# A low weight part formed by an accumulating DMA in every fourth half of a two-layer encoder's weight stream

## The chip, the cores and the metric

The kernel runs on one core of a Trainium2 chip. The metric is the device time of one execution in microseconds. The kernel before takes 2125.69 us (median of 3 runs, 2125.62 to 2129.74).

## What is computed

The reference is a two-layer encoder on one sequence of 256 tokens with 2048 features, in float32. Cut to what matters:

```python
for i in range(DEPTH):                      # DEPTH = 2
    h = rms_norm(x, attn_norm[i])
    if i % 2 == 0:                          # 8 heads on a 64-wide grid, 8 dilated heads
        x = x + even_mixer(h, even_w_in[j], even_rpb[j], even_w_out[j])
    else:                                   # 16 query heads, 4 key/value heads, window 128
        x = x + odd_mixer(h, odd_w_qkv[j], odd_sink[j], odd_w_out[j])
    x = x + sq_relu_mlp(rms_norm(x, mlp_norm[i]), w_mlp_in[i], w_mlp_out[i])
return rms_norm(x, final_norm)
```

All weights are used once. They make up most of the 382 MB that the kernel reads from HBM.

## The kernel before, in words

**Two exact parts.** Every float32 operand of a matmul is split in two: a high part that ScalarE (ACT) makes by copying to the type float32r, and a low part that VectorE (DVE) makes as the operand minus its high part (`split`, L80 to L82). A product is then three products: high by high, high by low, low by high. The activations keep their two parts side by side (`u`, `hid`, `o`, each with features on the partitions).

**The weight stream.** A unit is 16 tiles (k-tiles) of 128 x 128 weights, one output tile of 128 features. It comes in two halves of 8 k-tiles, 512 KB each. `need` puts the halves of all matrices on one list in the order of their use; `take_half` (L94 on) takes the next. It first fills a queue of loaded halves up to `AHEAD` + 1, and for each of these it issues the load on SP's queue (L98, tile `r`, 6 buffers), the copy `h<-r` on ACT (L81, 5 buffers) and the subtraction `l<-r,h` on DVE (L82, 5 buffers). `AHEAD` is 2. Of twelve units, the first ones after a phase in which activations become ready late, the second half has only 6 k-tiles in `h` and `l`; its last two go to tiles of their own.

**The products.** `k_range` (L134 on) issues two matmuls per k-tile on TensorE (PE): `h` against both activation parts at once (512 columns, L142) and `l` against the high part (256 columns, L144). `value_pair` (L253 on) uses the weights as the moving operand and works on two halves at a time (L264). `unit` takes a sum bank of three, `joined` empties it (ACT L171, DVE L173). Small work of attention and of the norms is put off by `later` and issued between k-tiles.

**Order.** The code's order is a priority: the framework plans times for all instructions when the program is built, and writes each engine's queue in the order of that plan. An instruction whose inputs are planned to be ready earlier can stand ahead of one that comes before it in the code (POOL issues `rev<-in_rpb`, L495, ahead of `sink_neg`, L448). On the chip each queue is then worked off strictly in its written order.

**The start.** Three units are loaded and multiplied in step with the activations (L440 to L465). GpSimd (POOL) loads small tables (L444 to L447). Before and between the first pairs of heads it makes the grid's bias for 8 heads, `make_grid_bias`: two loads `rev` on POOL's own DMA queue (L495, one buffer), then `rel<-rev,mask_a` (L497, four buffers), which waits for these. After the eighth `rel` POOL has no work. `norm_for_heads` makes the first norm: sums on PE (L202), the root on ACT (L205), a few small steps and a diagonal matrix on DVE (L213), then a product with it on PE (L217).

Of the kernel before, what the change touches and what calls it, by code (L numbers as in the profile page):

```python
# [7 lines left out]
F32 = mybir.dt.float32  # L8
F32R = mybir.dt.float32r
AF = mybir.ActivationFunctionType  # L10
ALU = mybir.AluOpType
# [15 lines left out]
HALF = KT // 2  # L27
RAW_BUFS = 6
PART_BUFS = 5
# steps between the stages of a head's attention  # L30
LAGS_0 = (5,4,3)
LAGS_1 = (4,5,3)
LAGS_END = (3,3,2)
# [7 lines left out]
def encoder(ctx: ExitStack, tc: tile.TileContext, a: dict, outT: bass.AP):  # L41
    nc = tc.nc
# [6 lines left out]
    work = ctx.enter_context(tc.tile_pool(name="work", bufs=3))  # L49
    acc_ps = ctx.enter_context(tc.tile_pool(name="acc_ps", bufs=3, space=PSUM))  # L50
    aux_ps = ctx.enter_context(tc.tile_pool(name="aux_ps", bufs=1, space=PSUM))

# [1 line left out]
    xs = const.tile([P, KT, T], F32, name="xs")  # L54
    u = const.tile([P, KT, 2, T], F32R, name="u")
    g = const.tile([P, 5, KT], F32, name="g")
# [15 lines left out]
    nc.vector.memset(eps, EPS)  # L72

    def warm(func, after):
        # has the function's table loaded ahead of its use
        nc.scalar.activation(warmed, after, func)

    warm(AF.Sqrt, eps)
# [1 line left out]
    def split(hi, lo, src):  # L80
        nc.scalar.activation(hi, src, AF.Copy)  # L81
        nc.vector.tensor_sub(lo, src, hi.bitcast(F32))  # L82

# [1 line left out]
    AHEAD = 2  # L85
    pending = []
    loaded = []

    def need(units, held=0):
        # of the first `held` units the last two k-tiles get tiles of their own  # L90
        for i, src in enumerate(units):
            pending.extend([(src[:, :HALF, :], HALF), (src[:, HALF:, :], HALF - 2 if i < held else HALF)])

    def take_half():  # L94
        while pending and len(loaded) <= AHEAD:
            src, n = pending.pop(0)
            r = raw.tile([P, HALF, P], F32, name="r")
            nc.sync.dma_start(r, src)  # L98
            h = whi.tile([P, HALF, P], F32R, name="h")
            l = wlo.tile([P, HALF, P], F32R, name="l")  # L100
            split(h[:, :n, :], l[:, :n, :], r[:, :n, :])
            tiles = [(h[:, k, :], l[:, k, :]) for k in range(n)]
            if n < HALF:
                h, l = (held_w.tile([P, 2, P], F32R, name=name) for name in ("hh", "hl"))
                split(h, l, r[:, n:, :])
                tiles += [(h[:, k, :], l[:, k, :]) for k in range(2)]
            loaded.append((h, l, tiles))
        return loaded.pop(0)

    def take_unit():  # L110
        return take_half()[2] + take_half()[2]

# [1 line left out]
    now = [0]  # L114
    tasks = []

# [8 lines left out]
    def tick():  # L125
        now[0] += 1
        run_due()

    def finish_tasks():
        while tasks:  # L130
            now[0] = max(now[0], tasks[0][0])
            run_due()
# [19 lines left out]
        done(ps)  # L152

    def some_units(done, act):
        # the last k-tiles of the activations become ready late: leave them for the end
        ps = [acc_ps.tile([P, 2 * T], F32, name="acc") for _ in done]
        parts = []
        for i in range(len(done)):
            parts.append(take_unit())
            if act is not u:  # L160
                assert heads_done >= set(range(KT - 2))
            k_range(ps[i], parts[i], act, range(KT - 2))
        if act is not u:
            finish_tasks()
        for i in range(len(done)):
            k_range(ps[i], parts[i], act, range(KT - 2, KT))
            done[i](ps[i])
# [5 lines left out]
        nc.vector.tensor_add(z, ps[:, :T], t)  # L173
        return z

# [1 line left out]
    def gained(k, which):  # L177
        x, gk = xs[:, k, :], g[:, which, k:k + 1]
        if which == 4:
# [14 lines left out]
    norm = {"ready": False, "waiting": []}  # L194

    def finish_norm(last=None, to=None):
        # mean square with tokens on partitions, 1/rms there, and the same along every partition
        ps = aux_ps.tile([P, 512], F32, name="m_ps", bufs=2)
        parts = [ssq] if last is None else [ssq, last]
        for j in range(2):  # L200
            for n, part in enumerate(parts):
                nc.tensor.matmul(ps[:, j:j + 1], part[:, j * P:(j + 1) * P], ones[:, 0:1],  # L202
                                 start=n == 0, stop=n == len(parts) - 1)
        r0, v, e = (work.tile([P, 2], F32, name=n, bufs=1) for n in ("r0", "v", "e"))
        nc.scalar.activation(r0, ps[:, :2], AF.Sqrt, bias=eps, scale=1.0 / D)  # L205
        nc.vector.tensor_scalar(v, ps[:, :2], 1.0 / D, EPS, op0=ALU.mult, op1=ALU.add)
        nc.vector.reciprocal(r0, r0)
        nc.vector.scalar_tensor_tensor(e, r0, -0.5, r0, op0=ALU.mult, op1=ALU.mult)
        nc.vector.tensor_mul(e, e, v)
        nc.vector.scalar_tensor_tensor(rcol, e, 1.5, r0, op0=ALU.add, op1=ALU.mult)  # L210
        diag = work.tile([P, 2, P], F32, name="diag", bufs=1)
        for j in range(2):
            nc.vector.tensor_scalar(diag[:, j, :], ident, rcol[:, j:j + 1], None, op0=ALU.mult)  # L213

        def along():
            out = aux_ps.tile([P, 512], F32, name="m_ps", bufs=2)
            nc.tensor.matmul(out[:, :T], ones, diag.rearrange("p j t -> p (j t)"), start=True, stop=True)  # L217
            to(out[:, :T])
        return along
# [13 lines left out]
        later(2, finish_norm(to=to))  # L233
        norm["ready"] = False

# [1 line left out]
    def head_parts(pool, name, bufs, scale, keep):  # L237
        def done(ps):
            z = joined(ps)
# [11 lines left out]
        return done  # L251

    def value_pair(pool, keep):  # L253
        # tokens on partitions, two heads at a time
        ps = acc_ps.tile([P, 2, T], F32, name="acc")
        for half in range(2):
            parts = [take_half()[:2] for _ in range(2)]
            for kk in range(HALF):
                k = half * HALF + kk
                h, l = (w.rearrange("p k c -> p (k c)")[:, (kk % 4) * T:(kk % 4 + 1) * T] for w in parts[kk // 4])  # L260
                for j in range(2):
                    js = slice(j * P, (j + 1) * P)
                    for n, (x, y) in enumerate(((0, h), (0, l), (1, h))):
                        nc.tensor.matmul(ps[:, j, :], u[:, k, x, js], y,  # L264
                                         start=k == 0 and j == 0 and n == 0,
                                         stop=k == KT - 1 and n == 2, skip_group_check=True)
                if kk % 2 == 1:
                    tick()
        assert norm["ready"]
        w = pool.tile([P, 2, 2, T], F32R, name="v", bufs=1)  # L270
        for j in range(2):
            nc.scalar.activation(w[:, 0, j, :], ps[:, j, :], AF.Copy, scale=rcol[:, j:j + 1])
            nc.vector.scalar_tensor_tensor(w[:, 1, j, :], ps[:, j, :], rcol[:, j:j + 1],
                                           w[:, 0, j, :].bitcast(F32), op0=ALU.mult, op1=ALU.subtract)
        keep.append(w)

    def attend(pool, o, head, q, k, v, side, biases, lags, sunk=False):
        """q, k, v: lists that hold the operands once their units are done."""
        def scores():
            if not q or not k:  # L280
                later(1, scores)
# [120 lines left out]
                    final = which_next == 4 and b == 1 and c == KT - 1  # L402
                    unit(added(c, final), hid, srcs=2, summed=final)

# [1 line left out]
    w0, w1 = a["even_w_in"], a["odd_w_qkv"]  # L406
    for p in range(8):
        base = 2 * p if p < 4 else 24 + 2 * (p - 4)
# [16 lines left out]
    need([a["odd_w_out"][c] for c in range(KT)], 3)  # L425
    mlp_units(1)

# [1 line left out]
    wps = aux_ps.tile([P, 512], F32, name="m_ps", bufs=2)  # L429
    for _ in range(10):  # L430
        nc.tensor.matmul(wps[:, :P], ones, ones, start=True, stop=True)

# [1 line left out]
    STARTERS = 3  # L434
    GROUPS = ((0, 2), (2, 4), (4, 8), (8, 12), (12, 16))
    starters = [[pending.pop(0)[0] for _ in range(2)] for _ in range(STARTERS)]
# [13 lines left out]
    for k0, k1 in GROUPS:  # L450
# [9 lines left out]
        for i in range(STARTERS):  # L460
            h, l = hl[i]
            for k in range(k0, k1):
                nc.tensor.matmul(sps[i], h[:, k % HALF, :], u[:, k].rearrange("p a t -> p (a t)"),
                                 start=k == 0, stop=False)
# [9 lines left out]
        later(1 + gi, some_squares(gi))  # L474
    later(8, norm_for_heads)

# [1 line left out]
    with tc.tile_pool(name="attn0", bufs=1) as pool:  # L478
        o = pool.tile([P, NH, 2, T], F32R, name="o")
        sl = slopes(8)  # L480
# [22 lines left out]
        for p in range(8):  # L503
            q, k, v = [[], []], [[], []], []
            for i in range(2):
                for j, (dst, name, sc) in enumerate(((q, "q", SCALE), (k, "k", 1.0))):
                    done = head_parts(pool, name, 2, sc, dst[i])
# [4 lines left out]
                h = 2 * p + i  # L512
# [7 lines left out]
        finish_tasks()  # L520
    mlp(0, 2)

# [1 line left out]
    with tc.tile_pool(name="attn1", bufs=1) as pool:  # L524
        o = pool.tile([P, NH, 2, T], F32R, name="o")
        sl = slopes(16)
        for p in range(2):
            k, v = [[], []], []
            done = [head_parts(pool, "k", 2, 1.0, k[i]) for i in range(2)]
# [7 lines left out]
            for i in range(8):  # L537
                h = 8 * p + i
                q = []
# [15 lines left out]

    mlp(1, 4)

# [1 line left out]
    def to(r):  # L559
        for k0, k1 in ((0, 1), (1, 2)) + tuple((k, k + 2) for k in range(2, KT, 2)):  # L560
            ks = slice(k0, k1)
            nc.vector.tensor_mul(xs[:, ks, :], xs[:, ks, :], r[:, None, :].to_broadcast([P, k1 - k0, T]))  # L562
            nc.sync.dma_start(outT[:, ks, :], xs[:, ks, :])
# [68 lines left out]
```

## Time and profile before

| | |
|---|---|
| median of 3 runs | 2125.69 us |
| the profiled execution | span 2127.8 us from first to last instruction (it has no other time of its own) |
| PE / PEld busy | 2104.8 us (99%) / 1852.0 us (87%) |
| DVE busy | 1340.4 us (63%) |
| ACT busy | 1035.6 us (49%) |
| POOL busy | 23.2 us (1%) |
| share of 16 DMA engines, loads on SP's queue | 53.2% |
| chain that ended last | PE 96%, DMA 2%, DVE 1% |

PE is TensorE's matmuls and PEld its weight loads, which overlap them. The chain is followed back from the last instruction to what released each step; its shares tell which engine the end depends on.

### The profile page before, as it was taken

The page shows a single profiled execution, that of the slowest core. Times are in us where ns is not written, and L with a number is a line of the kernel's source. Part 1 is how long each engine was busy: PE and PEld are TensorE (multiplying, and loading weights), DVE is VectorE, ACT ScalarE, POOL GpSimd, SP SyncE. Part 2 cuts the span into 40 slices and gives each one's busy share as a digit, 9 for nine tenths or more (in the row PEclk, how much of TensorE's full clock was granted, in tenths as well). Part 3 has the DMA queues.
Part 4 walks back from the last instruction along what each step waited for, and adds up shares of the span by engine and source line. Part 5 has one row for each costly group of instructions (what it writes and reads, how often), then busy time and mean ns, then how long its engine had stood idle before and what let it go on. Part 6 is the DMA issues. An engine that isn't in the chain of part 4 may idle for free.

```text
span 2127.8 us, 31825 instructions
## 1 busy us (share of the span) xinstructions
PE 2104.8 (99%) x12438; PEld 1852.0 (87%) x12438; DVE 1340.4 (63%) x2088; ACT 1035.6 (49%) x1602; POOL 23.2 (1%) x33
## 2 busy tenths in 40 slices
PE   8999999999999999999999999999999999999997
PEld 6999998888888888888888998888888888888887
DVE  6766676766655556665656877766655556665554
ACT  6555555544444444444445656544444444444442
POOL 2100000000000000000000000000000000000000
PEclk9999999999999999999999999999999999999998
DMA  9754455555555555555555444555555555555552
GB/s 258 180 171 168 168 170 176 190 180 188 187 187 188 188 186 185 187 187 189 188 188 187 148 162 143 188 185 188 185 187 187 188 188 186 187 188 188 188 188 90
DMA packets 108294, 386.06 MB, mean 181 GB/s; under 512 B 12352, under 2 KB 13392, under 8 KB 108144
## 3 DMA queue, kind: packets, MB, share of 16 engines
q1 hardware_dynamic: 106992, 381.73, 53.2%
q0 software_dynamic: 1008, 2.27, 1.5%
q8 instruction: 97, 1.59, 0.3%
q14 instruction: 53, 0.43, 0.1%
q10 hardware_dynamic: 144, 0.04, 0.0%
HBM read 381.89 MB, written 2.10 MB: 180 GB/s over the span
## 4 chain that ended last, share of the span: by engine, by line
PE 96%; DMA 2%; DVE 1%; SPq 0%; ACT 0%; issue 0%; DVEq 0%; ACTq 0%
PE acc L142 58%; PE acc L144 30%; PE acc L264 5%; PE s_ps L288 1%; PE m_ps L332 1%; DMA r<-in_even_w_in 1%; PE p_ps L313 1%; DMA r<-in_even_w_v 1%; DMA xs<-in_xT 0%; ACT h L81 0%; DVE l L82 0%; DVE xs L562 0%; SPq L440 0%; PE acc L140 0%; PE acc L139 0%
## 5 line engine op out<-in xcount | busy, mean ns | idle before, releaser
L82 DVE TENSOR_TENSOR l<-r,h 128x1024 fp32r<-128x1024 f32 (+3 forms) x729 | 880.8, 1209 | 718.4 <-ACT h L81 716.3
L81 ACT ACTIVATE h<-r 128x1024 fp32r<-128x1024 f32 (+3 forms) x729 | 761.5, 1045 | 985.3 <-PE acc L142 646.9
L142 PE MATMUL acc<-u,h 128*128 128x512 f32 x2820 | 1001.0, 397 | 0.0
L144 PE MATMUL acc<-u,l 128*128 128x256 f32 x2820 | 793.8, 281 | 0.0
L142 PE MATMUL acc<-hid,h 128*128 128x512 f32 x2016 | 705.8, 393 | 0.0
L142 PEld LDWEIGHTS acc<-u,h 128*128 128x128 f32 x2820 | 529.7, 188 | 126.9
L144 PE MATMUL acc<-hid,l 128*128 128x256 f32 x2048 | 571.5, 279 | 0.0
L144 PEld LDWEIGHTS acc<-u,l 128*128 128x128 f32 x2820 | 531.7, 189 | 0.2
L142 PEld LDWEIGHTS acc<-hid,h 128*128 128x128 f32 x2016 | 377.7, 187 | 90.3
L144 PEld LDWEIGHTS acc<-hid,l 128*128 128x128 f32 x2048 | 383.7, 187 | 0.0
L142 PE MATMUL acc<-o,h 128*128 128x512 f32 x500 | 176.2, 394 | 1.1 <-DVE z L173 1.1
L144 PE MATMUL acc<-o,l 128*128 128x256 f32 x500 | 139.6, 279 | 0.0
L264 PE MATMUL acc<-h,u 128*128 128x256 f32 x640 | 119.6, 283 | 0.0
L173 DVE TENSOR_TENSOR z<-acc,t 128x256 f32<-128x256 f32 x275 | 114.4, 418 | 2.2 <-ACT t L171 2.1
L142 PEld LDWEIGHTS acc<-o,h 128*128 128x128 f32 x500 | 93.7, 187 | 23.7 <-DVE z L173 1.7
L171 ACT ACTIVATE t<-acc 128x256 f32<-128x256 f32 x275 | 100.5, 366 | 5.5 <-PE acc L144 2.7
L264 PEld LDWEIGHTS acc<-h,u 128*128 128x128 f32 x640 | 100.9, 190 | 0.5
L144 PEld LDWEIGHTS acc<-o,l 128*128 128x128 f32 x500 | 93.7, 187 | 0.0
L264 PE MATMUL acc<-l,u 128*128 128x256 f32 x320 | 90.0, 281 | 0.0
L264 PEld LDWEIGHTS acc<-l,u 128*128 128x128 f32 x320 | 60.9, 190 | 0.1
L374 DVE SCALAR_TENSOR_TENSOR z<-z 128x256 f32<-128x256 f32 x128 | 54.4, 426 | 4.2
L82 DVE TENSOR_TENSOR hid<-z,hid 128x256 fp32r<-128x256 f32 x128 | 53.4, 419 | 1.3 <-ACT hid L81 1.2
(94 smaller groups left out, 859.3 us busy)
## 6 DMA issues: line engine op xcount, KB each, us to landing
r<-in_w_mlp_in SPq DMA_DIRECT2D x256, 512.0 KB, 4.2
r<-in_w_mlp_out SPq DMA_DIRECT2D x256, 512.0 KB, 4.5
r<-in_even_w_in SPq DMA_DIRECT2D x58, 512.0 KB, 3.8
r<-in_odd_w_qkv SPq DMA_DIRECT2D x40, 512.0 KB, 3.7
r<-in_even_w_v SPq DMA_DIRECT2D x32, 512.0 KB, 3.7
r<-in_even_w_out SPq DMA_DIRECT2D x32, 512.0 KB, 3.7
r<-in_odd_w_out SPq DMA_DIRECT2D x32, 512.0 KB, 3.7
r<-in_odd_w_v SPq DMA_DIRECT2D x8, 512.0 KB, 4.2
```

The costliest lines, as they stand in the source:

```text
L81: nc.scalar.activation(hi, src, AF.Copy)
L82: nc.vector.tensor_sub(lo, src, hi.bitcast(F32))
L142: nc.tensor.matmul(ps, h, act[:, k].rearrange("p a t -> p (a t)"), start=start, stop=False)
L144: nc.tensor.matmul(ps[:, :T], l, act[:, k, 0, :], start=False, stop=stop)
L171: nc.scalar.activation(t, ps[:, T:], AF.Copy)
L173: nc.vector.tensor_add(z, ps[:, :T], t)
L264: nc.tensor.matmul(ps[:, j, :], u[:, k, x, js], y, start=k == 0 and j == 0 and n == 0, stop=k == KT - 1 and n == 2, skip_group_check=True)
L288: nc.tensor.matmul(s_ps[:, i, :], qh[:, x, qs], kh[:, y, :], start=n == 0, stop=n == 2)
L313: nc.tensor.transpose(p_ps[:, j, i * P:(i + 1) * P], s[:, i, j * P:(j + 1) * P], ident)
L332: nc.tensor.matmul(o_ps[:, :T], vv[:, x, j, side * P:(side + 1) * P], pt[:, y, j, :], start=n == 0, stop=n == 5)
L374: nc.vector.scalar_tensor_tensor(z, z, 0.0, z, op0=ALU.max, op1=ALU.mult)
```

## The change

Two edits in the weight stream. `AHEAD` becomes 3, so that one more half is kept in the queue of loaded halves. And a counter runs over the halves that `take_half` prepares: for every fourth one, if it has all 8 k-tiles, ACT makes `h` as before and then also writes the negated high part into `l`; a DMA issued by POOL then adds the raw half `r` onto `l`, from SBUF to SBUF. The other halves keep the old path, and so do the three units of the start, which don't pass through `take_half`. The diff also takes out comments; that is left out here.

```diff
-    AHEAD = 2
+
+    AHEAD = 3
+    halves = [0]
     pending = []
     loaded = []
...
             h = whi.tile([P, HALF, P], F32R, name="h")
             l = wlo.tile([P, HALF, P], F32R, name="l")
-            split(h[:, :n, :], l[:, :n, :], r[:, :n, :])
+            halves[0] += 1
+            if n == HALF and halves[0] % 4 == 0:
+
+                nc.scalar.activation(h, r, AF.Copy)
+                nc.scalar.activation(l, h.bitcast(F32), AF.Copy, scale=-1.0)
+                nc.gpsimd.dma_start(l.bitcast(F32), r, accum_op=ALU.add)
+            else:
+                split(h[:, :n, :], l[:, :n, :], r[:, :n, :])
             tiles = [(h[:, k, :], l[:, k, :]) for k in range(n)]
```

## Rows read from the trace of the kernel before

**Rows 1.** The page: span, PE's busy time, and the clock in 40 slices.

```profile
span 2127.8 us, 31825 instructions
...
PE 2104.8 (99%) x12438; PEld 1852.0 (87%) x12438; DVE 1340.4 (63%) x2088; ACT 1035.6 (49%) x1602; POOL 23.2 (1%) x33
...
PEclk9999999999999999999999999999999999999998
```

**Rows 2.** Waits of PE, whole run: total us, times, longest us.

```profile
PE acc L463 <- ACT h L81: 6.2, 5, 1.8
PE m_ps L217 <- DVE diag L213: 4.8, 2, 3.1
PE acc L142 <- DVE z L173: 1.1, 2, 0.6
```

**Rows 3.** Windows: length, busy us by engine, PE's clock, DMA share, GB/s.

```profile
core 0: us, PE busy (x) PEld busy (x) DVE busy (x) ACT busy (x) POOL busy (x), PEclk, DMA share, GB/s
35.00:60.00 25.00, 21.89 (x149) 20.52 (x148) 18.43 (x35) 14.99 (x24) 5.08 (x6) 0.93 0.98 268
...
100.00:322.00 222.00, 222.00 (x1513) 204.01 (x1512) 150.01 (x272) 115.79 (x204) 0.00 (x0) 1.00 0.50 169
415.00:700.00 285.00, 285.00 (x1622) 247.99 (x1621) 170.86 (x233) 129.53 (x179) 0.00 (x0) 1.00 0.55 186
```

**Rows 4.** Timeline, 700 to 712 us: start, us, engine, line, operation [idle before, releaser].

```profile
700.71 1.06 ACT L81 ACTIVATE h<-r 128x1024 fp32r<-128x1024 f32 x1 [1.47 <-PE acc L142]
...
703.42 0.39 PE L142 MATMUL acc<-hid,h 128*128 128x512 f32 x1
...
703.50 1.06 ACT L81 ACTIVATE h<-r 128x1024 fp32r<-128x1024 f32 x1 [1.74 <-PE acc L142]
703.66 0.28 PE L144 MATMUL acc<-hid,l 128*128 128x256 f32 x1
...
703.78 0.39 PE L142 MATMUL acc<-hid,h 128*128 128x512 f32 x1
```

**Rows 5.** Groups by form: busy us, mean ns of one, idle before.

```profile
L82 DVE TENSOR_TENSOR l<-r,h 128x1024 fp32r<-128x1024 f32 x702 | 860.9, 1226 | 703.2 <-ACT h L81 701.4
...
L81 ACT ACTIVATE h<-r 128x1024 fp32r<-128x1024 f32 x702 | 743.6, 1059 | 964.0 <-PE acc L142 636.1 <-issue 294.8 <-PE acc L264 12.3
```

**Rows 6.** The page's DMA queues and issues, whole run.

```profile
q1 hardware_dynamic: 106992, 381.73, 53.2%
q0 software_dynamic: 1008, 2.27, 1.5%
...
r<-in_w_mlp_out SPq DMA_DIRECT2D x256, 512.0 KB, 4.5
```

**Rows 7.** Timeline of ACT, 30 to 58 us.

```profile
37.54 1.06 ACT L81 ACTIVATE h<-r 128x1024 fp32r<-128x1024 f32 x1 [0.21 <-DMA r<-in_even_w_v]
...
50.16 1.06 ACT L81 ACTIVATE h<-r 128x1024 fp32r<-128x1024 f32 x1 [5.11 <-DMA r<-in_even_w_in]
51.12 0.24 ACT L205 ACTIVATE r<-m_ps,eps 128x2 f32<-128x2 f32 x1
```

**Rows 8.** Timeline of PE, 40 to 62 us.

```profile
43.84 0.28 PE L264 MATMUL acc<-l,u 128*128 128x256 f32 x1
...
53.78 0.70 PE L217 MATMUL m_ps<-diag,ones 128*128 128x256 f32 x2 [3.11 <-DVE diag L213]
```

**Rows 9.** DMA issues in 30 to 60 us: KB each, median us to landing.

```profile
r<-in_even_w_in SPq DMA_DIRECT2D x8, 512.0 KB, 10.4
...
rev<-in_rpb POOLq DMA_DIRECT2D x4, 96.0 KB, 8.3
```

**Rows 10.** Timeline of POOL, whole run.

```profile
37.97 1.30 POOL L495 DMA_DIRECT2D rev<-in_rpb  x2 [0.29 <-POOL rel L497]
49.78 1.00 POOL L497 TENSOR_TENSOR rel<-rev,mask_a 128x384 f32<-128x384 f32 x1 [10.51 <-DMA rev<-in_rpb]
51.08 1.30 POOL L495 DMA_DIRECT2D rev<-in_rpb  x2 [0.29 <-POOL rel L497]
64.00 1.01 POOL L497 TENSOR_TENSOR rel<-rev,mask_a 128x384 f32<-128x384 f32 x1 [11.62 <-DVE st L293]
```

## The prediction

> **What bounds the kernel now.** I read the page's head and slices first, to see which engine is full and whether its clock is. The span is 2127.8 us, TensorE (PE) is busy in 2104.8 of it, and its granted clock is at nine tenths or more of the upper of its two levels (2.4 GHz) in all slices but the last [rows 1]. Next, who PE waits for in the whole run: the five waits of the first 35 us in the start's own products (6.2 us), two waits for the norm's diagonal matrix (4.8 us, one of them 3.1 us long) and two of 0.6 us for the projection sums [rows 2]. No row says that PE waits for a weight half's low part `l` once the start is over. Then the windows: in 100 to 322 us and in 415 to 700 us PE is busy for the whole stretch, at full clock, while the DMA engines are half used [rows 3]. Last a stretch of the steady stream: one k-tile is two matmuls, and the next k-tile's first starts 0.36 us after this one's (0.35 on average: the copies `h<-r`, one per half of 8 k-tiles, stand 2.79 us apart) [rows 4]. So PE streams at its own pace. The most that any edit of the weight preparation can give back is the waits behind the start, 3.1 and 1.1 us, and the 1.7 us that a stretch at the lower clock costs (25 us at a mean of 0.93 are 3.5 us at half clock [rows 3]). That is 5.9 us, 0.28%.
>
> **The sum's base.** Durations are from the profiled execution; its span of 2127.8 us is 2.1 above the median of the runs, 2125.69, and inside their scatter. I take the changes from that span and add them to the median. About 0.2% (4.3 us) is what a measurement of this kernel can tell from no change.
>
> **The parts.**
> How many: 714 halves pass through `take_half`; every fourth is 178. Seven of these are second halves of six k-tiles (of the 12 held units) and keep the old path: 171 accumulating DMAs of 512 KB.
>
> *Removed:* 171 subtractions on DVE of 1.226 us, 210 us of DVE time [rows 5]. Worth nothing: PE doesn't wait for them.
>
> *Added on ACT:* 171 copies with scale -1 of the same shape as `h<-r`, 1.06 us each, 181 us [rows 5]. ACT is idle before most of those copies until a PE matmul frees a buffer (1.74 us before the one at 703.50 [rows 4]), so the copy lies beside PE. The cover is the lead of a half: `h` and `l` have 5 buffers each, so half m starts when half m-5 is used up, and PE then works through four halves, 4 x 2.79 = 11.2 us, before it wants half m. One half more ahead (AHEAD 3) doesn't lengthen this, since the buffers set it: cost and gain nothing.
>
> *Added on POOL and the DMA engines:* after 2.1 us of ACT the DMA has 11.2 - 2.1 = 9.1 us to be issued, land and release PE. What such an accumulate takes no row shows. From below: a plain 512 KB load lands in 4.5 us [rows 6]. A packet of the loads takes 53.2% x 16 x 2127.8 us / 106,992 = 0.17 us [rows 6], 8 packets per engine and DMA. If the destination is read too, 8 more packets' time, 1.4 us; if every packet also waits for one of a load, another 1.4 us: 4.5 + 1.4 + 1.4 = 7.3 us, which I take, since size, memory and row length are those of the loads. From above: POOL's own queue took 1.5% x 16 x 2127.8 / 1008 = 0.51 us per packet [rows 6], in pieces much smaller than 4 KB; at that, 16 of them, 4.5 - 1.4 + 8.1 = 11.2 us, 2.1 us beyond the cover. I take the middle value: hidden, with 1.8 us to spare, from about 100 us on.
> The Trainium skill (DMA: Bandwidth & Descriptors, Anatomy of one DMA) gives about 2.0 us plus the bytes at 436 GB/s, 3.2 us for 512 KB, and Collectives: The Full Stack (Part 3) says that an add inside the DMA needs two source reads and so runs at half the rate; as an estimate that is 2.0 + 2.4 = 4.4 us, and by it the steady stream would be hidden with more to spare. The trace is above its figure for a plain copy already: 4.5 us for 512 KB [rows 6].
>
> *Moved:* `r` is now freed by the DMA's landing, not by DVE. Load m+6 waits for it, and SP's later loads stand behind that one: freed at 2.1 + 7.3 = 9.4 us after the half's start, landed 4.5 us later at 13.9, wanted six halves on, at 16.7. Hidden; what is late next, if the DMA takes over 10 us, is the load.
>
> *The start, where the cover is missing.* The fourth half of `take_half` is in the first value pair. Its `h` copy starts at 37.54 us [rows 7], when its load has landed. PE's first use of its `l` falls at 43.84 us [rows 8]. With the second copy the DMA can't be issued before 39.7 us: 4.2 us of cover instead of 9.1. And the stretch is crowded: in 35 to 60 us the DMA engines are 98% busy [rows 3], loads that elsewhere land in 4.5 us take 10.4, and the small bias loads `rev` of POOL's queue 8.3 [rows 9]. POOL has a third trouble: it issued `rev` at 37.97 us and then stood until 49.78 us for its landing before `rel`, and went on to the next pair of `rev` at 51.08 [rows 10]. An accumulate queued behind that `rel` is issued at about 51 to 52.4 us, lands 5.8 (7.3 without the contention that has gone by then) to 8 us later, at 57 to 60, and PE stands from 43.8: 13 to 16 us. Queued ahead of it, it is issued at 39.7, but behind two `rev` on POOL's rings, of which the trace has one landing at about 8.3 us after issue [rows 9]; with 10 to 12 us of its own it lands at 49.7 to 51.7: 6 to 8 us. Which order the planner writes, the trace can't tell; ACT shows that its times for these first loads are too short, for `h` at 50.16 stood 5.11 us for its load with the norm's root L205 queued behind it [rows 7].
> Against this: PE's later wait of 3.1 us for the norm [rows 8] falls away, since the norm's chain has time to catch up while PE stands. And a longer stand costs one or two more stretches at the lower clock, 1.7 us each as above. POOL's waits for the later `rel` (64.00 and on [rows 10]) may hold back the 16th and 20th half for 0 to 3 us.
> Sum of the start: behind `rel` 14.5 - 3.1 + 1.7 + 1 = +14 us; ahead of it 7 - 3.1 + 1 = +5 us. I can't choose by a row, so I take the middle, +9.5 us.
>
> **Sum.** 2125.7 + 0 (steady) + 9.5 (start) = 2135 us, 0.4% slower. This case's own range is 2129 to 2145.
>
> **Rivals.**
> *The accumulate outlasts its cover in the steady stream.* Each of the 171 then costs what it takes beyond 9.1 us. For: nothing here was yet moved from SBUF to SBUF with an add, and the upper bound of 11.2 us is beyond the cover; 2.1 x 171 = 360 us more, 2495 us. At 9.5 us it is 68 us and 2203. Against: load and accumulate differ in one extra read only.
>
> *The DMA engines fill up.* Loads take 53.2% now [rows 6]. 171 x 128 = 21,900 packets at two reads, 0.34 us, add 22%: 75%, not full. At twice 0.51 us they would add 65%: 118%, and the span would stretch to about 2127.8 x 1.18 = 2510 us.
> The Trainium skill (DMA: Bandwidth & Descriptors, Issuing engines are not separate DMA queues) says that DMAs of all queues run on the same 16 engines and interleave, which speaks against the change; the trace agrees so far as the loads land in 10.4 us beside POOL's queue and in 4.5 without it [rows 6, 9].
>
> *Not slower.* The place is PE's first use of the fourth half's `l`, 43.84 us. If the planner puts the accumulate ahead of `rel` and it lands by about 47 us, the stand is 3 us and is paid back by the norm's wait of 3.1 us, which PE then doesn't have; landing by 44 us even gives these 3.1 and 1.7 us of clock back: 2121 to 2129 us. It decides at a landing of about 7 us after issue. For: 7.3 us is what I take for the steady stream. Against: 98% busy DMA engines, and two `rev` ahead in the ring.
>
> *That the change doesn't do what it says:* if the saved DVE time mattered anywhere, it would be in attention; but PE is busy throughout 100 to 322 us [rows 3], so nothing comes of it. This is inside the forecast.
>
> **How the numbers follow.** Start stand with a hidden steady stream: 0.53. Outlasted cover: 0.21. Full DMA engines: 0.05. Not slower: 0.21, of which 0.04 are faster by over 0.2%, since that needs nearly all of the 5.9 us. So slower 0.53 + 0.21 + 0.05 = 0.79, same 0.17, faster 0.04. Range: from 2125 (leaving out the faster end) to 2200 (leaving out the outlasted cover from about 0.4 us per accumulate up, and the full DMA engines).
>
> **What would show it.** Right: after 100 us PE without gaps, L82 `l` some 171 fewer, 171 POOL issues of `l<-r` that land in 6 to 8 us, DMA near 75%; one PE wait of 5 to 16 us near 44 us that names `l`'s DMA, and no norm wait behind it. Wrong: PE waits for `l`'s DMA every fourth half (outlasted cover), DMA slices at 9 throughout (full engines), or a first accumulate that lands by 47 us (not slower).

## The result and the profile after

The changed kernel takes 2136.74 us (median of 4 runs, 2135.53 to 2137.10) against 2125.65 us (4 runs, 2124.75 to 2129.74) of the kernel before: a ratio of 1.0042 [1.0029, 1.0054], 11.1 us slower. Measured again later (below), it is 6.0 us slower, 1.0029 [1.0017, 1.0040]. The profiled execution of the changed kernel took 2137.1 us, of which 2135.2 are its span.

The page of the changed kernel, its parts on busy time, slices, queues, groups and DMA issues:

```profile
span 2135.2 us, 32285 instructions
...
PE 2106.6 (99%) x12438; PEld 1852.8 (87%) x12438; DVE 1140.6 (53%) x1917; ACT 1201.1 (56%) x1773; POOL 172.9 (8%) x204
...
PEclk8999999999999999999999999999999999999998
DMA  9977776778888787878787665778888887878884
...
q1 hardware_dynamic: 106992, 381.73, 52.1%
q0 software_dynamic: 25632, 91.93, 24.8%
...
L105 ACT ACTIVATE h<-r 128x1024 fp32r<-128x1024 f32 x171 | 181.2, 1060 | 225.2 <-PE acc L150 212.7
L107 POOL DMA_DIRECT2D l<-r x171 | 149.7, 875 | 1880.2 <-ACT l L106 1847.4
L106 ACT ACTIVATE l<-h 128x1024 fp32r<-128x1024 f32 x171 | 179.5, 1049 | 1.6
...
r<-in_w_mlp_out SPq DMA_DIRECT2D x256, 512.0 KB, 4.8
l<-r POOLq DMA_DIRECT2D x171, 512.0 KB, 4.7
```

PE is as full as before [rows 1]. DVE lost 200 us, ACT gained 166 us, and no wait of PE shows that either moved the end. POOL's queue, which the 171 accumulates go through, holds 24.8% of the 16 DMA engines' time instead of 1.5% [rows 6], and the accumulates land in 4.7 us in the median, like a plain load of the same size in this kernel (4.8 us). The waits of PE, whole run (total us, times, longest us):

```profile
PE acc L272 <- DMA l<-r: 7.8, 1, 7.8
PE acc L471 <- ACT h L81: 4.2, 5, 1.5
PE acc L471 <- DVE u L191: 2.3, 2, 1.9
PE m_ps L225 <- DVE diag L221: 1.7, 1, 1.7
```

Against [rows 2], behind the start's own products one long wait is new, a single one of 7.8 us for `l`'s DMA, and one has gone: of the two waits for the norm's diagonal matrix only the one at the end of the kernel is left (1.7 us); the 3.1 us of the start are not there. 170 of the 171 accumulates make PE wait for nothing. The windows (columns as in [rows 3]):

```profile
35.00:60.00 25.00, 17.20 (x102) 15.95 (x101) 10.98 (x18) 13.21 (x21) 7.18 (x8) 0.80 0.94 204
...
100.00:322.00 222.00, 222.00 (x1514) 204.31 (x1513) 130.96 (x253) 133.39 (x222) 16.19 (x19) 1.00 0.74 217
415.00:700.00 285.00, 285.00 (x1622) 247.85 (x1621) 143.60 (x214) 154.75 (x209) 21.32 (x25) 1.00 0.80 232
```

In both later windows PE is full at full clock, though the DMA engines went from 50 and 55% to 74 and 80%. Between 35 and 60 us PE works 4.7 us less than before, and the clock granted there is 0.80 instead of 0.93. Where that comes from, the timelines of POOL and PE show:

```profile
41.12 1.00 POOL L505 TENSOR_TENSOR rel<-rev,mask_a 128x384 f32<-128x384 f32 x1 [8.55 <-DMA rev<-in_rpb]
42.41 1.30 POOL L503 DMA_DIRECT2D rev<-in_rpb  x2 [0.29 <-POOL rel L505]
44.38 0.97 POOL L107 DMA_DIRECT2D l<-r  x1 [0.67 <-ACT l L106]
49.55 1.53 POOL L505 TENSOR_TENSOR rel<-rev,mask_a 128x384 f32<-128x384 f32 x1 [4.21 <-DMA rev<-in_rpb]
```

```profile
45.15 0.39 PE L272 MATMUL acc<-h,u 128*128 128x256 f32 x2
53.34 0.58 PE L272 MATMUL acc<-l,u 128*128 128x256 f32 x1 [7.80 <-DMA l<-r]
```

The planner put the accumulate of the fourth half ahead of the waiting `rel` (49.55) and behind two `rev` (42.41). It is issued at 44.38 us and lands 8.9 us later, and PE stands for it. After the stand PE's products with `l` take 0.41 to 0.58 us instead of 0.28, and PE is at the lower clock until 59.3 us, 6.0 us long. The difference of the two spans, 7.4 us, is made of these: +1.5 before the value products begin (they begin at 42.5 instead of 40.9 us; the first unit of the stream, ahead of them, at 36.7 instead of 35.2), +7.8 the stand, -3.1 the norm's wait, +1.3 the clock (6.0 us at half clock against 3.4 in the kernel before, half of each lost): 7.5 us. From the first product of layer 0's attention output to the last product of the second MLP the kernel before takes 1791.2 us and the changed one 1790.9. Nothing is lost or won there.

### The profile page after: what moved, and what is told of

The parts are those of the page before. It is cut to its first block, busy times and chain, and to the rows that moved or that the text cites. A ratio compares the mean times of both kernels' runs of the same rounds, so it can differ in the third digit from the quotient of the medians.

```text
span 2135.2 us, 32285 instructions
## 1 busy us (share of the span) xinstructions
PE 2106.6 (99%) x12438; PEld 1852.8 (87%) x12438; DVE 1140.6 (53%) x1917; ACT 1201.1 (56%) x1773; POOL 172.9 (8%) x204
## 3 DMA queue, kind: packets, MB, share of 16 engines
q0 software_dynamic: 25632, 91.93, 24.8%
## 4 chain that ended last, share of the span: by engine, by line
PE 96%; DMA 2%; DVE 1%; ACT 0%; issue 0%; DVEq 0%; SPq 0%
PE acc L150 58%; PE acc L152 30%; PE acc L272 5%; DMA xs<-in_xT 1%; PE m_ps L340 1%; PE s_ps L296 1%; PE p_ps L321 1%; DMA r<-in_even_w_v 0%; DMA l<-r 0%; DVE xs L570 0%; DVE l L82 0%; PE acc L148 0%; PE acc L147 0%; DMA g<-in_gains 0%; PE m_ps L225 0%; PE m_ps L210 0%
## 5 line engine op out<-in xcount | busy, mean ns | idle before, releaser
L82 DVE TENSOR_TENSOR l<-r,h 128x1024 fp32r<-128x1024 f32 (+3 forms) x558 | 670.4, 1202 | 786.2 <-ACT h L81 784.7
L81 ACT ACTIVATE h<-r 128x1024 fp32r<-128x1024 f32 (+3 forms) x558 | 580.1, 1040 | 594.7 <-PE acc L150 558.2
L105 ACT ACTIVATE h<-r 128x1024 fp32r<-128x1024 f32 x171 | 181.2, 1060 | 225.2 <-PE acc L150 212.7
L107 POOL DMA_DIRECT2D l<-r x171 | 149.7, 875 | 1880.2 <-ACT l L106 1847.4
L106 ACT ACTIVATE l<-h 128x1024 fp32r<-128x1024 f32 x171 | 179.5, 1049 | 1.6
```

The source lines that it names most:

```text
L105: nc.scalar.activation(h, r, AF.Copy)
L106: nc.scalar.activation(l, h.bitcast(F32), AF.Copy, scale=-1.0)
L107: nc.gpsimd.dma_start(l.bitcast(F32), r, accum_op=ALU.add)
```

## The experiments

### Where the loss is

My theory was that the whole loss is the fourth half's accumulate in the start. The rival: the 170 others, or `AHEAD`, cost something too. Three kernels part them; their edits, the first and third on the changed kernel, the second on the kernel before:

```diff
 e1: -  if n == HALF and halves[0] % 4 == 0:
     +  if n == HALF and halves[0] % 4 == 0 and halves[0] > 4:
 e2: -  AHEAD = 2
     +  AHEAD = 3
 e3: -  if n == HALF and halves[0] % 4 == 0:
     +  if n == HALF and halves[0] == 4:
```

> The accumulate is left out for the fourth half alone; the other 170 stay, and so does AHEAD 3. Theory (the whole loss is the one stand of PE at the fourth half, in the crowded start): about the time of the kernel before, 2126 us (2124 to 2130), no PE wait for l's DMA, and the norm's wait of about 3 us is back. Rival (the other 170 cost something each, by ACT's added copies or by DMA traffic): it stays near 2137 us.

Measured: 2130.15 us (11 runs) beside 2128.39 (26 runs of the kernel before), 1.0007 [0.9998, 1.0015], just above the theory's range. PE's wait near 45 us is gone and the norm's wait is back, at 4.4 us. The waits for `l<-r` are 0.5 and 0.3 us.

> AHEAD 3 alone, no accumulate at all. Theory (five buffers set the lead, not AHEAD): 2126 us (2124 to 2130), PE's waits as before. Rival (AHEAD 3 reorders the first loads and copies and so has a part in the loss): 2129 to 2134 us, with more waits of PE before 40 us.

Measured: 2128.96 us (12 runs), 1.0000 [0.9992, 1.0009]. `AHEAD` costs and gives nothing that these runs resolve.

> Only the fourth half is accumulated, the other 170 take the old path. Theory: the same time as the changed kernel, 2135 to 2138 us, with one PE wait of 6 to 9 us for l's DMA near 45 us. Rival (the 170 have a part): between 2126 and 2134 us.

Measured: 2134.28 us (8 runs), 1.0026 [1.0016, 1.0036]: 5.9 us for a single accumulate, with this wait of PE:

```profile
PE acc L272 <- DMA l<-r: 5.8, 1, 5.8
```

The time lies 0.7 us below the theory's range and just above the rival's. The stand was read from the fastest of the eight executions, 2130.59 us, so its 5.8 us needn't be that of the median.

The changed kernel was run again, beside the experiments of the next part:

> The changed kernel once more, beside the kernel before on this chip, as the yardstick for the other three. Theory (fourth half's stand about 6 us as measured alone, about 2 us more from the accumulates of the next 60 us): 7 to 10 us over the kernel before. Rival (the first comparison, 11 us between medians of 4, was the true size): 10 to 12 us over.

Measured: 2134.71 us (6 runs) beside 2128.67 (22 runs), 1.0029 [1.0017, 1.0040], with a stand of 8.1 us. That is less than the 7 to 10 us expected. The place of the loss is as the theory had it: the fourth half alone costs 5.9 us, the whole change 6.0 by the larger sample, and the change without the fourth half 1.8 with zero in its interval, so a part of 1 or 2 us for the other 170 is not excluded. The kernel before itself scatters from 2125.7 to 2132.4 us in those 22 to 26 runs, and three of its first four runs lay at or below the lower edge, while the changed kernel's first four had a median 2.0 us above that of its repeat; both fit the larger first ratio.

### What makes the start so tight

In the kernel before POOL's queue holds 33.1% of the DMA engines in 35 to 60 us, for two pairs of the small loads `rev`. If these are what keeps the accumulate and the weight loads from landing, moving them must shorten the stand and may help the kernel before too. With two buffers for `rel` instead of four, POOL's third `rel` waits for a buffer (until 59.8 us in the kernel before, 65.3 in the changed one), and the fourth pair of `rev` stands behind it:

```diff
-            rel = pool.tile([P, 6, GRID], F32, name="rel", bufs=4)
+            rel = pool.tile([P, 6, GRID], F32, name="rel", bufs=2)
```

On the changed kernel:

> The changed kernel with two buffers of rel in place of four: the fourth bias's two loads rev then stand behind the first scores, after 60 us, and POOL's ring is empty when the first accumulate is issued. Theory (the first accumulate lands late mainly because rev stands ahead of it in the ring): it lands in 5 to 7 us in place of 9, PE's wait near 45 us falls from 8 to 3 or 5, 2130 to 2134 us. Rival (the weight loads' crowd alone makes it late): landing still 8 to 9 us, 2135 to 2138 us.

Measured: 2131.68 us (11 runs), 1.0011 [1.0002, 1.0020]. The accumulate is issued at 41.18 us and lands in 7.3 us, between the two expectations (8.9 in the changed kernel's first profile, 11.4 in its repeat's). It is also issued earlier than in the first profile (44.38), so whether the `rev` ahead in POOL's queue or the crowd of all loads made the landing late isn't shown. PE stands less than half as long:

```profile
PE acc L272 <- DMA l<-r: 3.5, 1, 3.5
```

The loss of 3.0 us beside the kernel before hides that the smaller crowd helps the kernel before as well, as the next run shows.

On the kernel before:

> The kernel before with two buffers of rel: rev of the fourth and fifth head leave the stretch from 38 to 53 us. Theory (that stretch is bound by the DMA engines, and the norm's wait of 3 us follows from a weight load that lands 11 us after its issue): that load lands in 8 us or less, the wait falls to under 1 us and the lower clock behind it goes, 2 to 5 us under the kernel before. Rival (rev is too small a part): same time within 1 us.

Measured: 2124.63 us (11 runs), 0.9980 [0.9971, 0.9989], 4.0 us faster. Its DMA queues and issues in 35 to 60 us:

```profile
q1 hardware_dynamic: 1991, 7.24, 80.7%
q0 software_dynamic: 14, 0.01, 0.9%
...
r<-in_even_w_in SPq DMA_DIRECT2D x8, 512.0 KB, 6.0
```

and the same stretch of the kernel before:

```profile
q1 hardware_dynamic: 1726, 6.28, 64.9%
q0 software_dynamic: 193, 0.39, 33.1%
```

193 small packets held a third of the engines, and without them the weight loads land in 6.0 us instead of 10.4 [rows 9]; the norm's wait falls from 3.1 to 0.2 us. The Trainium skill (DMA: Bandwidth & Descriptors, Issuing engines are not separate DMA queues) says that DMAs run on the same 16 engines and interleave, whichever engine started them. The trace agrees: POOL's share went from 33.1 to 0.9% and that of the weight loads from 64.9 to 80.7%.

This run is also the like-for-like base of the one before it, and beside it the changed kernel with two `rel` buffers loses 7.1 us (2131.68 and 2124.63), no less than the 6.0 without the edit. The stand is shorter, but the norm's wait that a stand used to swallow is no longer there, and the stretch at the lower clock comes only with the stand: PE is at 0.93 of the clock in 35 to 60 us with the accumulate and at 1.00 without it.

The first two pairs of `rev` stand even earlier, among the start's own loads. A one-element copy from the last tile of the activations into `rev` makes POOL wait for these (on the kernel before, beside `bufs=2`):

```diff
             rev = pool.tile([P, 6, GRID], F32, name="rev", bufs=1)
+            if h == 0:
+                nc.gpsimd.tensor_copy(rev[:, 0, 0:1], xs[:, KT - 1, 0:1])
```

> As the run before it, and the very first rev also waits until the last activations have landed (a one-element write into its buffer), so that no rev runs in the first 27 us. Theory (the start is bound by the DMA engines and rev takes its share): PE's waits in its first 35 us and the stretch at the lower clock shrink, the first unit of the stream begins 1 to 4 us earlier, 3 to 8 us under the kernel before. Rival (rev then only moves into the stretch of 30 to 55 us, where the norm waits): same time within 1.5 us, the norm's wait 3 to 5 us.

Measured: 2119.22 us (5 runs), 0.9959 [0.9945, 0.9972], 9.5 us faster for both edits together, 5.4 of it by the second; the theory had 3 to 8. The first 35 us in the windows, first of `rel` with two buffers alone, then of this kernel:

```profile
0.00:35.00 35.00, 27.86 (x113) 21.80 (x114) 21.08 (x46) 20.53 (x47) 8.89 (x17) 0.80 0.93 234
```

```profile
0.00:35.00 35.00, 30.52 (x160) 25.39 (x161) 25.51 (x54) 25.25 (x55) 8.45 (x15) 1.00 0.94 295
```

At nearly the same busy share (0.94 and 0.93) the DMA engines move 295 instead of 234 GB/s. The weight pieces of 256 KB land in 6.8 us, 10.6 in the kernel before; PE does 160 matmuls instead of 113, at full clock throughout, and the first unit of the stream begins at 28.1 us, in the kernel before at 35.2. So where the small loads stand costs the start more (9.5 us) than the accumulate does (6.0, beside the same runs of the kernel before). It was run once more:

> The kernel before with the late first rev once more, beside the same with accumulates. Theory: 2117 to 2122 us, as in its first run. Rival (the first gain was a chance of the start's scatter): within 3 us of the kernel before.

Measured: 2118.56 us (5 runs), 0.9959 [0.9947, 0.9972].

### How much room the steady stream has

Here the theory was that the accumulate fits into its cover and that the room runs out only if it takes longer or comes oftener. More often first, from the 25th half on, so that the start is the old one but for `AHEAD`:

```diff
 e4:  -  if n == HALF and halves[0] % 4 == 0:
      +  if n == HALF and halves[0] % 2 == 0 and halves[0] > 24:
 e11: -  if n == HALF and halves[0] % 4 == 0:
      +  if n == HALF and halves[0] % 3 == 0 and halves[0] > 24:
```

> From the 25th half on every second half is accumulated, none before: twice the accumulating traffic, none in the start. At 24.8% of the DMA engines for 171 the load would be 52 + 48 = 100%. Theory (a cover of 9 us against 4.7 us to landing, the DMA engines are the next bound): the DMA slices go to 9, landings stretch to 7 to 10 us, PE waits now and then, 2130 to 2250 us. Rival (the spare cover swallows it): 2126 us with no waits for l's DMA. Rival (ACT with two more copies per four halves, or POOL's queue, bounds): PE waits while DMA slices stay at 7 to 8.

Measured: 2155.21 us (2 runs), 1.0126 [1.0108, 1.0143], 26.8 us slower. The page's queues and DMA issue, PE's wait and a window:

```profile
q1 hardware_dynamic: 106992, 381.73, 50.3%
q0 software_dynamic: 48960, 176.88, 45.0%
...
l<-r POOLq DMA_DIRECT2D x333, 512.0 KB, 6.9
```

```profile
PE acc L152 <- DMA l<-r: 11.8, 19, 2.5
```

```profile
415.00:700.00 285.00, 283.85 (x1621) 247.18 (x1620) 116.37 (x192) 179.45 (x233) 42.64 (x49) 1.00 1.00 276
```

The two queues hold 95% of the engines, the median accumulate needs 6.9 us instead of 4.7, and PE waits for 19 of 333. The waits sum to 11.8 of the 26.8 us. Two new waits of 2.5 and 1.7 us in attention's end add to them, and PE's own busy time is 6.2 us longer (2111.0 against 2104.8); where that comes from I haven't laid to rows. With full engines in mind as the cause, every third half should have been almost free:

> As every second half from the 25th on, but every third: some 226 accumulates and about 52 + 33 = 85% of the DMA engines. Theory (loss comes only when the DMA engines are full): landings of 5 to 6.5 us, no or very few PE waits for l's DMA, 2126 to 2132 us. Rival (loss grows with the number of accumulates): half of what every second half cost, 2135 to 2145 us.

Measured: 2158.67 us (2 runs), 1.0143 [1.0124, 1.0162]. That is a miss: with 226 accumulates and the DMA engines at 0.86 in 415 to 700 us it loses as much as every second half does, and PE's waits for `l<-r` are longer:

```profile
PE acc L152 <- DMA l<-r: 18.2, 16, 4.0
```

They sum to 18.2 of the 30.2 us lost. So the mean share isn't what decides. The longest stand, in the timelines of ACT, POOL and PE:

```profile
1395.73 0.42 ACT L81 ACTIVATE hh<-r 128x256 fp32r<-128x256 f32 x1 [7.69 <-DMA r<-in_w_mlp_in]
...
1401.67 0.87 POOL L107 DMA_DIRECT2D l<-r  x1 [11.79 <-ACT l L106]
...
1410.82 0.39 PE L152 MATMUL acc<-u,l 128*128 128x256 f32 x1 [3.97 <-DMA l<-r]
```

ACT waited 7.69 us for a weight load, with the next accumulate's copies behind it. This load was late because an accumulate holds its raw buffer until it has landed: the one issued at 1379.50 took 10.2 us, SP stood 7.1 us for it, and the load went out at 1389.7. ACT's wait then made the ordinary subtractions late, SP stood 8.0 us for one of these, and three loads went out within 2 us (1398.65 to 1400.57). The next accumulate is issued late (1401.67) and lands among them after 9.1 us. This is read from one stand of 16, and it doesn't say why every third half loses as much as every second: SP's waits for `l<-r` sum up to 736.8 us here, 389.8 in the changed kernel and 1261.8 with every second half. That stays open. What the spacing by three changes, that accumulates then fall on both halves of a unit in turn, wasn't tried by itself.

Then longer: a second accumulating DMA adds a tile of zeros, so that the chain has twice its length (every fourth half from the 25th on; `rel` has three buffers to make room for the zeros):

```diff
                 nc.gpsimd.dma_start(l.bitcast(F32), r, accum_op=ALU.add)
+                nc.gpsimd.dma_start(l.bitcast(F32), zeros, accum_op=ALU.add)
```

> From the 25th half on, every fourth half is accumulated, and a second accumulating DMA of the same size adds zeros onto the same l, issued when the first has landed; rel has three buffers to make room for the zeros. Theory (a half's cover is 11.2 us from the freed buffer, of which ACT's two copies take 2.1): the chain is 2.1 plus two landings of 4.7 to 5.5 us, 11.5 to 13.1 us, so that each of some 165 halves costs PE 0.3 to 1.9 us: 2175 to 2440 us, with PE waits for l's DMA in nearly every fourth half. Rival (the cover is longer than worked out, or something else paces the halves): under 2140 us, few waits.

Measured: 2869.05 us (2 runs), 1.3481 [1.3456, 1.3505]. The direction is the theory's, the size is far beyond it. PE's wait and POOL's timeline over one of the stands:

```profile
PE acc L155 <- DMA l<-zeros: 544.1, 81, 9.0
```

```profile
814.95 0.87 POOL L109 DMA_DIRECT2D l<-r  x1 [11.07 <-ACT l L108]
820.17 0.87 POOL L110 DMA_DIRECT2D l<-zeros  x1 [4.35 <-DMA l<-r]
826.14 0.87 POOL L109 DMA_DIRECT2D l<-r  x1 [5.10 <-ACT l L108]
834.55 0.87 POOL L110 DMA_DIRECT2D l<-zeros  x1 [7.54 <-DMA l<-r]
```

The DMA of zeros issued at 820.17 lands 10.6 us later, beside four weight loads issued between 817.6 and 823.2; PE stands 6.8 us for it. The next accumulate's zeros are held in POOL's queue until 834.55, since that accumulate's first DMA, issued at 826.14, has to land first. So about every second accumulate costs some 7 us, 567 us of stands in all. The granted clock falls to a mean of 0.887, and PE's busy time is 175 us longer than in the kernel before (2280.0 and 2104.8); the two make up the 741 us. My forecast had left out the clock and the loads that a stand itself bunches.

### Without the start

Last, the changed kernel with the late `rev`, two `rel` buffers and accumulates from the 25th half on (165 of them):

> The changed kernel with the late first rev and two buffers of rel, its accumulates from the 25th half on. Theory (past the start the accumulates cost and give nothing): the time of the late rev without any accumulate, 2119 us (2117 to 2122), 0.4% under the kernel before. Rival (the accumulates of the steady stream cost a few us): 2122 us or more. Rival (DVE freed by the accumulates gives something back once the start is short): under 2117 us.

Measured: 2119.38 us (5 runs), 0.9961 [0.9947, 0.9974], next to 2118.56 of the kernel before with the same two edits of the start. PE has no wait for `l<-r`, and the window is full:

```profile
415.00:700.00 285.00, 285.00 (x1622) 248.11 (x1621) 140.63 (x206) 153.06 (x202) 21.54 (x25) 1.00 0.81 233
```

Past the start the accumulates cost nothing and give nothing that these runs resolve. The fastest version of this study is the kernel before with the late `rev` and two `rel` buffers, 2118.6 to 2119.2 us, 0.41% faster than the kernel before and faster than the changed one.

## Why the prediction was right, and where its terms were off

**The bound.** PE streams at its own pace and no edit of the weight preparation speeds it up: right. DVE's 200 us gave nothing, and ACT's two copies took 181.2 and 179.5 us (forecast 181 for the added one) without a wait of PE behind them. `AHEAD` is worth nothing (second experiment).

**The steady stream.** Hidden, as forecast, and shown twice: by equal times between the first attention output product and the last MLP product, and by the version without the start. The term of the accumulate itself was too large: 4.7 us to landing, not 7.3. It lies 0.2 us above the lower bound, a plain load's 4.5 [rows 6]; of the two additions of 1.4 us, the second read and the contention, next to nothing shows in the landing. The second read is there all the same, in the packets: 24.8% x 16 x 2135.2 us less the kernel before's 1.5% x 16 x 2127.8 us of POOL's queue [rows 6] are 7962 us in 24,624 packets, 0.32 us each (forecast 0.34), twice a load's. The sum came out the same, since either value lies within the cover of 9.1 us. By the Trainium skill (Collectives: The Full Stack, Part 3), with the rate halved, the estimate was 4.4 us; the trace agrees with the doubled reads by its packet time, while the landing of 4.7 us doesn't show a halved rate, since a plain load takes 4.8 us beside it. The DMA engines' share was forecast at 75%; the two queues hold 76.9%.

**The start.** The place, the cause and the signs were right: one stand at PE's first use of the fourth half's `l`, no norm wait behind it, a few us more at the lower clock. For the order on POOL I could choose by no row and took the middle of two branches, +9.5 us. That this middle, 2135 us, lies so near the 2136.74 first measured is luck, since neither branch gives it. The planner wrote the branch "ahead of `rel`", for which the working gave +5 us: a stand of 6 to 8 us (7.8, 8.1 and, alone, 5.8 were measured), 3.1 back, 1 for the clock (1.3). The repeat's +6.0 and the +5.9 of the fourth half alone lie by that branch; the first comparison's +11.1 lies above the middle. Of that, 7.5 us are laid to rows in the profiled execution, and 1.5 of these came ahead of the first accumulate. In the repeat's profile the branch's steps came as forecast, an issue at 40.4 us (39.7) and a landing 11.4 us later (10 to 12):

```profile
40.38 0.97 POOL L107 DMA_DIRECT2D l<-r  x1 [1.01 <-ACT l L106]
51.87 0.58 PE L272 MATMUL acc<-l,u 128*128 128x256 f32 x1 [8.07 <-DMA l<-r]
```

In the first profile the fourth half's `h` copy began only at 41.9 us after its load (37.5 in [rows 7]), and the accumulate took 8.9 us; the two differences offset each other.

**The term of 0 to 3 us for the 16th and 20th half** behind POOL's later `rel` wasn't seen: the changed kernel has no second wait for `l<-r`.

**The rivals.** The outlasted cover (0.21) is not there at one accumulate in four, as the landing is half the cover. It appears with a chain twice as long: there the two DMAs land in 5.4 and 8.2 us (medians), 13.6 us together, and the rival's formula gives 165 x (13.6 - 9.1) = 743 us; measured were 741. The agreement is partly chance, since that time is made of stands and of the lower clock behind them, which the formula doesn't know. Full DMA engines (0.05) appear at one in two, with 26.8 us lost; that they are the cause there isn't shown, since one in three loses as much at 0.86. Between them lies what no rival named, read from one stand at one in three: raw buffers held until the accumulate lands, and loads in bursts behind them. "Not slower" (0.21) needed a landing by 47 us; it came at 53.3. With two `rel` buffers the landing came at about 48.5 us and the stand was 3.5 us, near what this rival asked for. Even so the change cost 7.1 us beside its own base: the norm's wait of 3.1 us that was to pay the stand back went with the same crowd. So a shorter stand alone wouldn't have made this rival right.

## What to carry to other kernels

An engine's time saved off the critical path is worth nothing, and work moved onto DMA queues should be judged where its cover is shortest: here one of 171 moves, the first, made all of the loss that could be resolved. A shorter stand isn't the whole answer either, when what shortens it also removes the wait that the stand used to cover. Before adding a transfer to a crowded start, look at which small loads stand there and can wait: moving them gained 9.5 us where the change lost 6.0. And a share of DMA time below 1 doesn't show that there is room: at 0.86 this kernel lost 30.2 us, and in the one stand that was read a transfer held a buffer and the loads queued behind it.

## What the runs showed that I had not expected

An accumulating DMA of 512 KB within SBUF lands as soon as a plain load from HBM (4.7 and 4.8 us in one kernel), at twice the packet time. 193 packets of POOL's small loads held 33.1% of the DMA engines' time in 25 us, 0.69 us each, while the 1726 of the weight loads held 64.9%, 0.15 us each. Accumulates in every third half cost as much as in every second (1.0143 and 1.0126), though they leave the engines at 0.86 instead of 1.00.
